# Attention stage of a decoder layer: every step with a q projection also gets one quarter of a u tile, and u is made by halves of the positions

## The chip, the cores and the metric

One core of one Trainium2 chip. The time is that of the device for one execution of the whole kernel, in microseconds (us), as the median of several runs. A profile of one execution shows each engine: PE (TensorE matmul; PEld is its weight load), DVE (VectorE), ACT (ScalarE), POOL (GpSimd) and SP (SyncE, which here issues DMAs).

## The reference

One decoder layer in float32 for 1024 positions of width 1024. What matters here is the input projection and the two token mixers:

```
h = rmsnorm(x)
[q | k | v | u | s | gate_a | gate_b] = h @ w_in      # in the kernel: q, k, v, u (512 wide), v_s (512 wide)
A = sliding_window_attention(q, k, v)                  # 8 heads of 64, window 128, ALiBi, a sink per head
B = gelu(u) * (tril(W_s) @ rmsnorm(gelu(v_s)) + b)     # in chunks of 128 positions
x = x + (sigmoid(gate_a) * (A @ w_oa) + sigmoid(gate_b) * (B @ w_ob)) @ w_out
x = x + down(silu(conv_g) * conv_v)                    # conv of width 3 over up(rmsnorm(x)), 2 x 2816 wide
```

## The kernel before

A product in float32 is made of three matmuls of a reduced float32: each operand is split into a high part (a copy by ACT, `copy_hi`) and a low part (a subtraction by DVE or POOL), and `mm3` adds high x high, high x low and low x high (lines 93 to 95).

The kernel is written out in one order by hand: each engine works its instructions in the order in which the code issues them. The change is in the attention stage, a loop of 20 steps (`for n in range(20)`). Attention step n < 16 is half of the heads (n // 8) for one block of 128 queries (n % 8). Its parts are spread over the steps:

- step n: `s_mm` (PE, the scores, PSUM tile `sc`; lines 439, 442), `s_mask` (DVE, lines 457 and 458, tile `c`), `s_max` (DVE, lines 465 to 467)
- step n + 1: `s_exp` (ACT exponentials, DVE sum and reciprocal, lines 479 and 480, POOL product, line 481)
- step n + 2: `p_trans` (PE transposes, tile `pt`), `p_split` (ACT `ch`, DVE `cl` in line 496, and four POOL selects that part the two key blocks, lines 503 and 505)
- step n + 4: `pv_mm` (PE, tile `pv`), `pv_out` (ACT and DVE, line 530, into `ya`). After the last step of each half `ya` is stored by SP (line 533).

Between these parts PE gets filling work, two slots to a step, from the table `FILL`: `q` is the q projection of a later attention step (24 matmuls of 256 columns), `u` one of 16 chunks of the u projection (12 matmuls of 512 columns), and `v` one half of the v_s projection of 128 positions (24 matmuls of 256 columns). The first slot stands ahead of `p_trans`, the second behind it. There are 12 `q`, 16 `u` and 4 `v`.

u has four tiles of 128 channels and 1024 positions. A chunk takes two of the eight k slices for all positions, so four chunks fill one PSUM tile `pu` of two banks, which DVE then evacuates in one instruction of 1024 columns (line 679). `pu` and the score tiles `sc` come from the same pool `psA` with two buffers of two banks: while a `pu` is being filled, the scores have one buffer.

`WHEN` names the step at whose end the weights of a later part are split; POOL makes the low part (line 110 for u, line 193 for q and v_s: `wv` and `wvB`). In step 15 SP begins to load x again (`rows_again`, tile `xa`, line 617); the second four rows of it are loaded behind the stage, into the buffer that `ya` leaves. ACT scales them (`x_gain`, line 631). Behind the stage `v_phase` finishes v_s (tile `pvs`, weights `wvB`), takes its GELU on ACT and its norm on DVE, and mixes (tile `pm`, seeded by ACT in line 926 and evacuated by DVE in line 943).

Of the kernel before, what the change touches and what calls it, by code (L numbers as in the profile page):

```python
# [14 lines left out]
ALU = mybir.AluOpType  # L15
# [12 lines left out]

ROWS = (slice(0, 64), slice(64, 128))
X_AHEAD = 5  # L30
FILL = "qu|q|qu|qu|uu|q|qu|qu|q|qu|qu|qu|q|uu|u|u|uu|vv|v|v".split("|")
WHEN = {"u1": 0, "q0": 1, "q1": 2, "u2": 5, "u3": 9, "v0": 13, "v1": 14, "z0": 16, "z1": 17}


# [7 lines left out]
def body(ctx, tc, nc, a):  # L42
    L, H = slice(0, 512), slice(512, 1024)
# [11 lines left out]
    def Y(s, dt=R, shape=None):  # L55
        return big.tile(shape or [128, 4, 1024], dt, tag="Y", name=nm(s), bufs=7)
# [16 lines left out]
    def PS(s):  # L73
        if psum.get("next"):
            return psum["next"].pop(0).tile([128, 1024], F, tag="P", name=nm(s))
        pools_ = psum["P"]
        pools_.append(pools_.pop(0))
        return pools_[-1].tile([128, 1024], F, tag="P", name=nm(s))
# [12 lines left out]
    def mm3(out, wh, wl, mh, ml, first, last, **kw):  # L91

        nc.tensor.matmul(out, wh, mh, start=first, stop=False, **kw)  # L93
        nc.tensor.matmul(out, wh, ml, start=False, stop=False, **kw)  # L94
        nc.tensor.matmul(out, wl, mh, start=False, stop=last, **kw)  # L95
# [21 lines left out]
    rstd_b = base.tile([128, 1024], F, name="rstd_b")  # L117
# [61 lines left out]
    def hx(j, k, c):  # L179

        h = c.start // 512
        return xq[k // 4][h][:, j, k % 4, c.start - 512 * h:c.stop - 512 * h]
# [44 lines left out]
    for k in range(8):  # L227
# [8 lines left out]
        for s in range(8):  # L236
            o = pkv[s // 4][:, (s % 4) * 256:(s % 4 + 1) * 256]
            c = slice(s * 128, (s + 1) * 128)
# [24 lines left out]
    def q_proj(n):  # L263
        half, b = divmod(n, 8)
        w = wq[half]
        p = PH("pq")[:, 0:256]
        c = slice(b * 128, (b + 1) * 128)
        for k in range(8):
            mm3(p, hx(0, k, c), hx(1, k, c), w[:, 0, k, :], w[:, 1, k, :], k == 0, k == 7)
        st[("pq", n)] = p  # L270
# [155 lines left out]
    uT = Y("uT", F)  # L426


    def s_mm(n):
        b = n % 8  # L430
        qs = st.pop(("qT", n))
        p = PS("sc")
        k0 = max(b - 1, 0) * 128
        ks = slice(k0, k0 + 256)
        for t2 in range(2):
            c = slice(t2 * 128, (t2 + 1) * 128)
            o = [p[:, (2 * g + t2) * 256:(2 * g + t2 + 1) * 256] for g in range(2)]
            for g in range(2):
                nc.tensor.matmul(o[g], qs[:, g, c], kTh[:, g, ks], start=t2 == 0, stop=False,
                                 skip_group_check=True)  # L440
            for g in range(2):
                nc.tensor.matmul(o[g], qs[:, g, c], kTl[:, g, ks], start=False, stop=True,
                                 skip_group_check=True)
        st[("ps", n)] = p.rearrange("p (h k) -> p h k", k=256)

    def s_mask(n):

        half, b = divmod(n, 8)
        p4 = st.pop(("ps", n))
        hs = slice(4 * half, 4 * half + 4)  # L450
        c = tm.tile([128, 4, 128], F, tag="c", name=nm("c"), bufs=3)
        if b == 0:
            nc.vector.tensor_tensor(c, p4[:, :, 0:128], ali[:, hs, :], op=ALU.add)
            nc.gpsimd.affine_select(out=c, in_=c, pattern=[[0, 4], [-1, 128]], compare_op=ALU.is_ge,
                                    fill=NEG, base=0, channel_multiplier=1)
        else:
            nc.vector.copy_predicated(p4[:, :, 128:256], msk, p4[:, :, 0:128])
            nc.vector.tensor_tensor(c, p4[:, :, 128:256], ali[:, hs, :], op=ALU.add)
        st[("c0", n)] = c

    def s_max(n):
        hs = slice(4 * (n // 8), 4 * (n // 8) + 4)
        c = st.pop(("c0", n))
        sm = tm.tile([128, 4, 4], F, tag="sm", name=nm("sm"), bufs=3)
        nc.vector.tensor_reduce(sm[:, 0, :], c, axis=AX.X, op=ALU.max)
        nc.vector.scalar_tensor_tensor(sm[:, 0, :], sm[:, 0, :], -1.0, nsink[:, hs], op0=ALU.mult, op1=ALU.min)
        nc.vector.tensor_tensor(sm[:, 2, :], sink_b[:, hs], sm[:, 0, :], op=ALU.add)
        st[("c", n)] = (c, sm)
# [3 lines left out]
    def s_exp(n):  # L472
        c, sm = st[("c", n)]
        m, den, es = sm[:, 0, :], sm[:, 1, :], sm[:, 2, :]
        for i in range(4):
            last_exp[0] = nc.scalar.activation(c[:, i, :], c[:, i, :], AF.Exp, bias=m[:, i:i + 1],
                                               accum_out=den[:, i:i + 1])
        nc.scalar.activation(es, es, AF.Exp)
        nc.vector.tensor_tensor(den, den, es, op=ALU.add)
        nc.vector.reciprocal(den, den)  # L480
        nc.gpsimd.tensor_tensor(c, c, den.unsqueeze(2).to_broadcast([128, 4, 128]), op=ALU.mult)
# [28 lines left out]
    def pv_mm(n):  # L510
        parts = st.pop(("p", n))
        p = PH("pv")
        ops = [(part[2], part[j]) for j in (0, 1) for part in parts[::-1]]
        for i, (kb, w) in enumerate(ops):
            for g in range(2):
                o = p[:, g * 256:(g + 1) * 256].rearrange("p (h q) -> p h q", q=128)
                nc.tensor.matmul(o, vhl[:, kb, g, :], w[:, 2 * g:2 * g + 2, :], start=i == 0 and g == 0,  # L517
                                 stop=i == len(ops) - 1, skip_group_check=True)
        st[("pv", n)] = p.rearrange("p (g h q) -> p g h q", g=2, q=128)
# [15 lines left out]
    ust = {("w", 0): tuple(u_next)}  # L535

    def u_chunk(i):
        t, j = divmod(i, 4)
        if j == 0:
            ust["p"] = PS("pu")  # L540
        p, (wh, wl) = ust["p"], ust[("w", t)]
        for k in (2 * j, 2 * j + 1):
            for h in range(2):
                c = slice(h * 512, (h + 1) * 512)
                mm3(p[:, c], wh[:, k, :], wl[:, k, :], hx(0, k, c), hx(1, k, c), k == 0, k == 7)
        return t if j == 3 else None

    n_q, n_u, n_v, u_done = [4], [0], [0], []
    pvs = {}

    def v_half(s, h):
        if h == 0:
            pvs[s] = PS("pvs")[:, 0:512] if s < 2 else PH("pvs")
        c = slice(s * 128, (s + 1) * 128)
        for k in range(8):
            mm3(pvs[s][:, 256 * h:256 * h + 256], hx(0, k, c), hx(1, k, c), wv[h][:, 0, k, :],
                wv[h][:, 1, k, :], h == 0 and k == 0, k == 7, skip_group_check=True)

    def filler(n, i):

        kind = FILL[n][i:i + 1]
        if kind == "q":
            q_proj(n_q[0])
            n_q[0] += 1
            return [n_q[0] - 1]
        if kind == "v":
            v_half(n_v[0], 0)
            n_v[0] += 1
        if kind == "u":
            t = u_chunk(n_u[0])  # L570
            n_u[0] += 1
            if t is not None:
                u_done.append((t, ust["p"]))
        return []

    wv = []
# [36 lines left out]
    def rows_again(r):  # L613

        t = Y("xa", F)
        for k in range(4):
            nc.sync.dma_start(t[:, k, :], a["xw"][4 * r + k, :, 257:1281])
        xr_raw.append(t)
# [24 lines left out]

    assert "".join(FILL).count("u") == 16 and "".join(FILL).count("q") == 12
    man = tc.manual_schedule()
    man.__enter__()
    for n in range(20):
        if n < 16:
            s_mm(n)
            s_mask(n)  # L650
        if 0 <= n - 1 < 16:
            s_exp(n - 1)
        if n < 16:
            s_max(n)
        if 0 <= n - 4 < 16:
            pv_mm(n - 4)
        q_new = filler(n, 0)
        if 0 <= n - 2 < 16:
            p_trans(n - 2)
        filler(n, 1)  # L660
        if 0 <= n - 4 < 16:
            pv_out(n - 4)
        for q in q_new:
            q_sq(q)
            q_ms(q)
        if 0 <= n - 2 < 16:
            p_split(n - 2)
        weights(n)
        if n == 15:
            rows_again(0)  # L670
        if n == 17:
            x_gain(0, (0, 1))
        if n == 18:
            x_gain(0, (2, 3))
            x_sums((0, 1), True)
        if n == 19:
            x_sums((2, 3), True)
        for t, p in u_done:
            nc.vector.tensor_tensor(uT[:, t, :], p, rstd_b, op=ALU.mult)
        u_done.clear()  # L680
        if n + 2 < 16:
            q_trans(n + 2)
            q_split(n + 2)
        for q in [3] + q_new if n == 0 else q_new:
            q_norm(q)
# [1360 lines left out]
```

## Time and profile before

| | us |
|---|---|
| three runs | 1184.26, 1184.44, 1184.85 |
| median | 1184.44 |
| span of the profiled execution, first to last instruction | 1183.5 |
| median less span (launch and end of an execution) | 0.9 |
| PE busy | 1170.3 (99% of the span) |
| attention stage, 48.93 to 182.10 | 133.17 |
| of which PE busy | 130.07 |

The profiled execution's own time is listed only as its span; what lies around it is 0.9 us, if it ran like the median. PE is busy for nearly the whole span, so the kernel's time is the time of its matmuls plus the waits of PE.

### The profile page before, as it was taken

What the parts mean: (1) busy time and instruction counts of PE and PEld (TensorE: products, weight loads), DVE (VectorE), ACT (ScalarE), POOL (GpSimd) and SP (SyncE); (2) the same over time, 40 slices, a digit from 0 to 9 for tenths busy, and PEclk for the clock granted to TensorE, in tenths of its full rate; (3) what the DMA queues carried; (4) which work ended last, traced back from release to release, by engine and by line L of the source; (5) the groups of instructions that cost most, each with busy time, mean ns of one, the idle gap of its engine ahead of it and who ended that gap; (6) DMA issues with size and microseconds to landing.
All of it is one profiled execution on the core that took longest, in us unless ns stands there. A gap on an engine that the chain in (4) does not pass through costs nothing.

```text
span 1183.5 us, 15928 instructions
## 1 busy us (share of the span) xinstructions
PE 1170.3 (99%) x5842; PEld 990.4 (84%) x5842; DVE 874.5 (74%) x1037; ACT 566.5 (48%) x878; POOL 631.8 (53%) x435
## 2 busy tenths in 40 slices
PE   8999999999999999999999999999999999999998
PEld 8989989988888878888878888888888888888887
DVE  7798975743536776678788788877888797875674
ACT  8555667644336653335444443444444445425331
POOL 2467685488884764444867677776767541000000
PEclk9999999999999999999999999999999999999999
DMA  7110136157556654454545445455555268975471
GB/s 272 37 55 19 54 130 228 56 168 239 161 160 204 233 193 154 146 176 132 138 129 169 118 149 152 142 141 134 166 137 160 72 219 287 365 232 196 155 231 67
DMA packets 80942, 188.66 MB, mean 159 GB/s; under 512 B 9184, under 2 KB 16864, under 8 KB 80736
## 3 DMA queue, kind: packets, MB, share of 16 engines
q1 hardware_dynamic: 73008, 167.58, 40.7%
q0 software_dynamic: 7456, 15.73, 8.0%
q10 hardware_dynamic: 400, 4.33, 1.1%
q8 instruction: 46, 0.75, 0.3%
q14 instruction: 32, 0.26, 0.1%
HBM read 146.97 MB, written 49.02 MB: 166 GB/s over the span
## 4 chain that ended last, share of the span: by engine, by line
PE 82%; DVE 4%; POOL 3%; ACT 2%; issue 2%; DMA 1%; DVEq 0%; POOLq 0%; SPq 0%; ACTq 0%
PE pz L1060 50%; PE pd L1855 10%; PE pdy L1855 8%; PE px L95 2%; PE px L93 2%; PE px L94 2%; PE pu L95 1%; PE pu L93 1%; PE pu L94 1%; PE pv L517 1%; PE pq L93 1%; PE pq L95 1%; PE pq L94 1%; DVE xa L621 1%; DMA lq<-wup 0%
## 5 line engine op out<-in xcount | busy, mean ns | idle before, releaser
L1060 PE MATMUL pz<-T,qh 128*128 128x512 f32 x472 | 145.6, 390 | 0.0
L1060 PE MATMUL pz<-B,ph 128*128 128x512 f32 x352 | 109.7, 393 | 0.7 <-ACT x L1695 0.7
L1060 PEld LDWEIGHTS pz<-T,qh 128*128 128x128 f32 x472 | 88.4, 188 | 18.6 <-ACT u L885 0.3
L1019 POOL TENSOR_TENSOR pl<-lp,ph 128x1024 fp32r<-128x1024 f32 x30 | 73.2, 2439 | 52.9 <-ACT ph L89 52.9
L1060 PE MATMUL pz<-T,ql 128*128 128x512 f32 x236 | 91.8, 389 | 0.0
L1019 POOL TENSOR_TENSOR ql<-lq,qh 128x1024 fp32r<-128x1024 f32 x30 | 76.8, 2559 | 9.1 <-ACT qh L89 9.1
L1060 PEld LDWEIGHTS pz<-B,ph 128*128 128x128 f32 x352 | 65.1, 188 | 16.7 <-ACT x L1695 3.8
L1078 DVE TENSOR_TENSOR pz<-pz,rstd_b 128x1024 f32<-128x1024 f32 x60 | 73.9, 1232 | 4.6 <-ACT rstd_b L143 2.5
L1060 PE MATMUL pz<-T,s3h 128*128 128x512 f32 x232 | 71.4, 389 | 0.0
L1060 PE MATMUL pz<-y,wjh 128*128 128x512 f32 x224 | 69.5, 391 | 0.6 <-POOL y L1233 0.3
L1060 PE MATMUL pz<-B,pl 128*128 128x512 f32 x176 | 68.6, 390 | 0.0
L1855 PE MATMUL pd<-bh,ah 128*128 128x512 f32 x176 | 68.5, 389 | 0.0
L1855 PE MATMUL pd<-bl,ah 128*128 128x512 f32 x176 | 68.5, 389 | 0.0
L1855 PE MATMUL pd<-bh,al 128*128 128x512 f32 x176 | 68.5, 389 | 0.0
L1060 PE MATMUL pz<-T,AX 128*128 128x512 f32 x264 | 63.4, 389 | 0.0
L1060 PE MATMUL pz<-B,AX 128*128 128x512 f32 x264 | 63.4, 389 | 0.0
L1019 POOL TENSOR_TENSOR s3l<-lq,s3h 128x512 fp32r<-128x512 f32 x20 | 26.0, 1298 | 62.3 <-ACT s3h L89 62.3
L1060 PEld LDWEIGHTS pz<-T,AX 128*128 128x128 f32 x264 | 49.5, 188 | 10.3
L1060 PEld LDWEIGHTS pz<-B,AX 128*128 128x128 f32 x264 | 49.6, 188 | 10.3
L89 ACT ACTIVATE AX<-lr 128x1024 fp32r<-128x1024 f32 x22 | 23.4, 1063 | 70.9 <-POOL lr L621 70.9
L621 DVE TENSOR_TENSOR pz<-pz,u 128x512 f32<-128x512 f32 x37 | 25.9, 700 | 42.5 <-ACT u L1072 36.2
L1550 DVE SCALAR_TENSOR_TENSOR tg<-pz,cp,tg 128x1023 f32<-128x1023 f32 (+1 forms) x44 | 56.2, 1278 | 0.8
(359 smaller groups left out, 3597.6 us busy)
## 6 DMA issues: line engine op xcount, KB each, us to landing
lp<-wup SPq DMA_DIRECT2D x22, 512.0 KB, 3.8
lq<-wup SPq DMA_DIRECT2D x22, 512.0 KB, 4.2
ra<-wdown SPq DMA_DIRECT2D x44, 256.0 KB, 4.9
b<-T SPq DMA_DIRECT2D x44, 256.0 KB, 3.5
lq<-wup POOLq DMA_DIRECT2D x42, 256.0 KB, 5.3
B<-tv SPq DMA_DIRECT2D x33, 256.0 KB, 2.0
T<-tt SPq DMA_DIRECT2D x33, 256.0 KB, 2.1
b<-B SPq DMA_DIRECT2D x33, 256.0 KB, 3.0
```

What stands on the lines that cost most here:

```text
L89: return nc.scalar.activation(dst, src, AF.Copy, scale=scale)
L93: nc.tensor.matmul(out, wh, mh, start=first, stop=False, **kw)
L94: nc.tensor.matmul(out, wh, ml, start=False, stop=False, **kw)
L95: nc.tensor.matmul(out, wl, mh, start=False, stop=last, **kw)
L517: nc.tensor.matmul(o, vhl[:, kb, g, :], w[:, 2 * g:2 * g + 2, :], start=i == 0 and g == 0, stop=i == len(ops) - 1, skip_group_check=True)
L621: eng.tensor_tensor(out, x, y, op=op)
L1019: nc.gpsimd.tensor_tensor(l, r, h.bitcast(F), op=ALU.subtract)
L1060: nc.tensor.matmul(o, p[:, k, :], m, start=not more and k == 0 and j == 0, stop=k == nk - 1 and j == 2, skip_group_check=True)
L1078: nc.vector.tensor_tensor(z, z, rstd_b, op=ALU.mult)
L1550: nc.vector.scalar_tensor_tensor(t[:, j:], p[:, 0:1024 - j], cw[:, ci, 2 - j:3 - j], t[:, j:], op0=ALU.mult, op1=ALU.add)
L1855: nc.tensor.matmul(o[d], p[:, k - k0, m], q[:, k - k0, :], start=new and k == 0 and j == 0, stop=k == HK - 1 and j == 2, skip_group_check= ...
```

## The change

`FILL` is rewritten: steps 0 to 11 all get `qu`, steps 12 to 15 one `u` each, steps 16 and 17 one `v` each, step 18 `vv` and step 19 nothing. A chunk of u now takes four of the eight k slices for 512 positions, so two chunks fill one bank; the pairs go through the first and the second 512 positions of each tile. One `pu` tile of two banks is held from the first chunk to the sixteenth, and each filled half is evacuated by an instruction of 512 columns while the other half is being filled.

```diff
-FILL = "qu|q|qu|qu|uu|q|qu|qu|q|qu|qu|qu|q|uu|u|u|uu|vv|v|v".split("|")
+FILL = "qu|qu|qu|qu|qu|qu|qu|qu|qu|qu|qu|qu|u|u|u|u|v|v|vv|".split("|")
...
     def u_chunk(i):
-        t, j = divmod(i, 4)
-        if j == 0:
+
+        t, h, j = i // 4, i // 2 % 2, i % 2
+        if i == 0:
             ust["p"] = PS("pu")
-        p, (wh, wl) = ust["p"], ust[("w", t)]
-        for k in (2 * j, 2 * j + 1):
-            for h in range(2):
-                c = slice(h * 512, (h + 1) * 512)
-                mm3(p[:, c], wh[:, k, :], wl[:, k, :], hx(0, k, c), hx(1, k, c), k == 0, k == 7)
-        return t if j == 3 else None
+        wh, wl = ust[("w", t)]
+        c = (L, H)[h]
+        p = ust["p"][:, c]
+        for k in range(4 * j, 4 * j + 4):
+            mm3(p, wh[:, k, :], wl[:, k, :], hx(0, k, c), hx(1, k, c), k == 0, k == 7)
+        return (t, c, p) if j else None
...
         if kind == "u":
-            t = u_chunk(n_u[0])
+            u = u_chunk(n_u[0])
             n_u[0] += 1
-            if t is not None:
-                u_done.append((t, ust["p"]))
+            if u:
+                u_done.append(u)
+            if n_u[0] == 16:
+                del ust["p"]
...
-        for t, p in u_done:
-            nc.vector.tensor_tensor(uT[:, t, :], p, rstd_b, op=ALU.mult)
+        for t, c, p in u_done:
+            nc.vector.tensor_tensor(uT[:, t, c], p, rstd_b[:, c], op=ALU.mult)
```

On PE, step 13 of the program before, from the end of its `pv` to the scores of step 14 (a run of like matmuls is left out at each line of dots; `pqt` is the transposed q of a later step):

```order
L517 MATMUL pv_1951<-cl_1818,vhl 128x256 x2
L93 MATMUL pu_1691<-x_5_118,wuh_1191 128x512
...
L487 MATMUL pt_1972<-ident,c_1738 128x128 x4
L93 MATMUL pu_1691<-x_5_118,wuh_1191 128x512
...
L295 MATMUL pqt_2010<-ident,qr_1925 128x128 x2
L439 MATMUL sc_2018<-kT_107,qs_1920 128x256 x2
```

The same step of the changed program:

```order
L517 MATMUL pv_1989<-cl_1876,vhl 128x256 x2
L93 MATMUL pu_735<-x_5_118,wuh_1670 128x512
...
L487 MATMUL pt_2010<-ident,c_1796 128x128 x4
L295 MATMUL pqt_2036<-ident,qr_1894 128x128 x2
L439 MATMUL sc_2044<-kT_107,qs_1960 128x256 x2
```

The second chunk of u has gone from this step to an earlier one, and the matmuls follow each other from `pt` to the scores of the next step.

On PE, the end of the stage before, from the `pv` of attention step 14 to the first matmul of `v_phase` (the one with `wvB`):

```order
L517 MATMUL pv_2306<-cl_2210,vhl 128x256 x2
L93 MATMUL pvs_2315<-wv_2004,x_3_116 128x256
...
L517 MATMUL pv_2349<-cl_2293,vhl 128x256 x2
L93 MATMUL pvs_2358<-wv_2004,x_3_116 128x256
...
L93 MATMUL pvs_2232<-wvB_2219,x_3_116 128x256
```

And in the changed program:

```order
L517 MATMUL pv_2307<-cl_2241,vhl 128x256 x2
L93 MATMUL pvs_2316<-wv_2030,x_3_116 128x256
...
L93 MATMUL pvs_2341<-wv_2030,x_3_116 128x256
...
L517 MATMUL pv_2375<-cl_2294,vhl 128x256 x2
L93 MATMUL pvs_2201<-wvB_2246,x_3_116 128x256
```

Both `v` of the end stand ahead of the `pv` of attention step 15 now, and none stands between it and `v_phase`.

## Rows read from the trace of the kernel before

A row of a stretch gives its length, then the busy us (and instructions) of PE, PEld, DVE, ACT and POOL, PE's granted clock, the DMA share and GB/s. A timeline's row gives start us, duration us and the instruction.

**Rows 1.** The profile's page: the span, and each engine's busy share.
```profile
span 1183.5 us, 15928 instructions
PE 1170.3 (99%) x5842; PEld 990.4 (84%) x5842; DVE 874.5 (74%) x1037; ACT 566.5 (48%) x878; POOL 631.8 (53%) x435
```

**Rows 2.** The attention stage in one stretch: us and busy us (instructions) by engine.
```profile
48.93:182.10 133.17, 130.07 (x920) 119.10 (x918) 113.36 (x240) 82.69 (x256) 92.01 (x99) 1.00 0.18 62
```

**Rows 3.** Timeline of PE: start us, duration us, instruction, [idle before it <-releaser].
```profile
83.05 0.47 PE L439 MATMUL sc<-kT,qs 128*128 128x256 f32 x2 [0.41 <-DVE uT L679]
179.02 0.51 PE L517 MATMUL pv<-cl,vhl 128*128 128x256 f32 x2 [0.54 <-POOL cl L505]
```

**Rows 4.** Timeline of PE: first score matmul of steps 1, 3, 4, 10, 12, 14, 15, then the next phase.
```profile
55.69 0.48 PE L439 MATMUL sc<-kT,qs 128*128 128x256 f32 x2
67.61 0.48 PE L439 MATMUL sc<-kT,qs 128*128 128x256 f32 x2
74.77 0.48 PE L439 MATMUL sc<-kT,qs 128*128 128x256 f32 x2
119.05 0.48 PE L439 MATMUL sc<-kT,qs 128*128 128x256 f32 x2
135.09 0.48 PE L439 MATMUL sc<-kT,qs 128*128 128x256 f32 x2
148.60 0.48 PE L439 MATMUL sc<-kT,qs 128*128 128x256 f32 x2
153.66 0.48 PE L439 MATMUL sc<-kT,qs 128*128 128x256 f32 x2
182.10 0.28 PE L93 MATMUL pvs<-wvB,x 128*128 128x256 f32 x1
```

**Rows 5.** Groups of DVE instructions by line in the stage: xcount | busy us, mean ns.
```profile
L458 DVE TENSOR_TENSOR c<-sc,ali 128x512 f32<-128x512 f32 x14 | 9.7, 691 | 0.6
L679 DVE TENSOR_TENSOR uT<-pu,rstd_b 128x1024 f32<-128x1024 f32 x4 | 4.9, 1215 | 0.0
```

**Rows 6.** Timeline of DVE in steps 12 to 14.
```profile
137.48 0.69 DVE L457 COPY_PREDICATED sc<-msk,sc 128x512 f32<-128x512 uint8 x1
144.06 0.69 DVE L457 COPY_PREDICATED sc<-msk,sc 128x512 f32<-128x512 uint8 x1
148.58 0.69 DVE L496 TENSOR_TENSOR cl<-pt,ch 128x512 fp32r<-128x512 f32 x1
152.66 1.08 DVE L479 TENSOR_TENSOR sm<-sm 128x4 f32<-128x4 f32 x1
```

**Rows 7.** Timeline of POOL at the end of the stage.
```profile
151.30 2.43 POOL L193 TENSOR_TENSOR wv<-v,wv 128x1024 fp32r<-128x1024 f32 x1
172.56 0.64 POOL L505 TENSOR_SCALAR_AFFINE_SELECT cl<-cl 128x512 fp32r<-128x512 f32 x1
```

**Rows 8.** SyncE's and ScalarE's timelines behind the stage.
```profile
181.28 0.80 SPq L533 DMA_DIRECT2D ya<-ya  x2
191.11 2.18 ACT L631 ACTIVATE xa<-xa,cp 128x1024 f32<-128x1024 f32 x2
```

**Rows 9.** The reload of x (tile xa), two first issues and their landing times.
```profile
L617 SPq DMA_DIRECT2D xa<-xw x2: 333/378/423, 185.6 to 186.0; - x2
DMA to landing us min/median/max: 3.6/4.7/5.7
```

**Rows 10.** Behind the stage: a link of the chain that ended last; PE's timeline.
```profile
191.21 2.08 ACT xa L631 x2
...
218.26 0.39 PE L93 MATMUL pm<-wgh,vsh 128*128 128x256 f32 x1 [0.52 <-ACT pm L926]
```

**Rows 11.** Kernel start: a PE wait, then two stretches with granted clock (third number from the end).
```profile
6.30 0.38 PE L93 MATMUL pkv<-wkv,x 128*128 128x256 f32 x1 [1.89 <-ACT x L89]
...
5.00:10.00 5.00, 3.64 (x17) 3.03 (x18) 3.24 (x7) 4.01 (x9) 0.00 (x0) 0.82 0.96 353
10.00:15.00 5.00, 5.00 (x38) 5.00 (x38) 5.00 (x11) 5.00 (x11) 0.00 (x0) 0.84 1.03 399
```


## The prediction

> **What bounds the kernel now.** I read the page first: PE is busy 99% of a span of 1183.5 us [rows 1], so time can only come from, or go into, PE's waits. Then the attention stage alone, from the first score matmul (48.93 us) to the first matmul that uses the second half of the w_v weights (182.10 us): 133.17 us with 130.07 busy [rows 2], so 3.10 us of it are idle. The waits of PE in that stage are small and of two kinds [rows 3]: in the steps that follow a step without a `u`, it waits a few tenths for DVE (0.41 us for the 1024-column evacuation `uT`, for instance), and near the end it waits for POOL, for the selects that cut the probabilities before the `pv` matmuls (0.54 us, tile `cl`). Last, the chain behind the stage: at 218.26 us PE waits 0.52 us for ScalarE's `pm` [rows 10], and the chain of waits that led there leaves PE for ScalarE and DVE well before, with the scaling of x at 191.21 us as one link of it [rows 10]. So there PE has no spare time to give: what ScalarE loses at 191 us, PE loses at 218 us.
>
> **The change part by part.**
>
> *Matmuls.* The same ones, in another order. No PE time is added or removed.
>
> *Steps 0 to 11 become uniform ("qu").* Such a step takes 8.02 us: steps 10 and 11 lie between 119.05 and 135.09 [rows 4]. Without its `pv` it takes 7.16 us, as step 3 does (67.61 to 74.77). Step 1 begins at 55.69 us as before. Steps 1 to 3 then take 3 x 7.16, less some 0.4 for the transposes that step 1 lacks (an estimate: 4 of its 50-odd matmuls), 21.1 us; step 4, with half a `pv`, 7.6; steps 5 to 11, 7 x 8.02 = 56.1. So step 12 begins at 55.7 + 21.1 + 7.6 + 56.1 = 140.5 us with no wait on the way, where it begins at 135.09 now with less work behind it. I cost these steps at no wait: steps 10 and 11 already are of this form, with one score buffer free, and they show none.
>
> *One score buffer all the time.* The score matmuls of a step need the mask and add of the step before (DVE, 0.69 each [rows 5, 6]) to be done. At least 4 us of other PE work lie between them even in a step with a single `u` (5.06 us from 148.60 to 153.66, less about 1 for the scores [rows 4]). Cost nothing; from the other side, 0.41 us at each place where DVE is late [rows 3].
>
> *Evacuations.* Eight of 512 columns in place of four of 1024. The 1024 form takes 1.215 us, a 512-column add out of PSUM 0.691 [rows 5]: 8 x 0.691 - 4 x 1.215 = 0.7 us more DVE time, spread over seven quiet steps and step 15. Nothing on the path, and the 0.41 us wait for the long one goes.
>
> *The end of the stage, which decides.* Steps 12 to 15 now have one `u` and nothing else, about 5 us of PE each, and steps 16 to 19 have `v`, `v`, `vv` and nothing. The work of DVE and POOL per step stays. So I follow POOL. In step 12 DVE starts its mask at step start + 2.39 us (135.09 to 137.48 [rows 4, 6]); this is the same afterwards. One step of DVE is 6.58 us there (137.48 to 144.06), of which 1.07 belong to a q (its three small instructions): 5.5 afterwards. From that mask to the `cl` subtraction in the same step are 4.52 us (144.06 to 148.58), with about 0.6 of waits for POOL: 3.9 to 4.5 afterwards. From this subtraction to the POOL instruction that makes the low part of `wv` are 2.72 us (148.58 to 151.30 [rows 6, 7]). So this first `wv` instruction starts at 2.4 + 5.5 + 3.9 + 2.7 = 14.5 us behind step 12's start, at 155.0 us (upper bound 155.6, from the 4.5; lower 154.0, if DVE were not behind PE at all). From there the order of POOL and DVE is the same in both kernels up to the end of the `cl` select of attention step 14: 151.30 to 172.56 + 0.64, 21.9 us. In that stretch POOL hardly rests and PE is early with all that it hands over, so I carry the 21.9 over whole: `cl` of step 14 is ready at 176.9 us. Then PE has the last pair of `pv` (0.4), two `v` (2.73 each: 182.10 - 179.02 - 0.35 [rows 3, 4]) and the `pv` of step 15 (0.9): the next phase begins at 176.9 + 0.4 + 5.5 + 0.9 = 183.7 us, **1.6 us later** than the 182.10 of now. The waits that went in the early steps come back, and more, as waits for POOL in steps 16 to 18.
>
> One instruction in that chain is worth a look. DVE's small product `sm` (L479) takes 1.08 us and ends at 153.74, just when POOL's `wv` instruction (151.30 + 2.43) ends [rows 6, 7]; I take it as held until then, as part of the 21.9. By my times POOL is first there by some 0.8 us (14.5 against about 15.3 us behind step 12). If DVE came first, what is held now would not be: 14.5 + 2.43 - 15.3 = 1.6 us would go out of the chain (a rival, below). The Trainium skill, page "SBUF — State Buffer", section "Who interferes with whom", has such a rule: a DVE instruction with two SBUF inputs and a GpSimd instruction that reads SBUF exclude each other for the whole instruction, and whichever issues first has its way. By that rule the trace agrees for the one order that it shows.
>
> *What hangs on the `pv` of step 15.* Now a `v` (2.73 us) lies between it and the next phase; afterwards none. Its result goes through ScalarE and DVE to `ya`, and SyncE stores `ya` (181.28 us [rows 8], 2.26 us behind the last pair at 179.02 [rows 3]). Behind that store, on the same queue, stands the reload of four rows of x (tile `xa`), which takes the buffer of `ya` and so waits until the store has landed; its first two issues are at 185.6 and 186.0 us and land 3.6 and 5.7 us later [rows 9], at 189.2 and 191.7. Afterwards the last pair is at 183.7 - 0.35 = 183.35, the store at 185.6, 4.3 us later, so the second row of x lands at 196.0. ScalarE scales the two rows from 191.11 us on, 1.09 each [rows 8]; moved by 1.6 us it would want the second row at 191.11 + 1.09 + 1.6 = 193.8. It waits **2.2 us**, and everything behind it on ScalarE with it: the GELU of the third v chunk, for which DVE waits, and so on up to `pm` and PE at 218 us, where there is no slack [rows 10]. Bounds: nothing, if the stores and loads land sooner on a freer queue; 3 us, if all four rows matter.
>
> **Sum.** 1.6 + 2.2 = +3.8 us on the profiled span of 1183.5 us, 1187.3; the runs' median, 1184.44, stands 0.9 above that span: **1188.2 us**.
>
> **The rivals.**
> - *POOL does not hold PE (faster).* From step 15 on (153.66 to 182.10 [rows 4], 28.4 us with its waits) PE now has three `u` and four `v` left. Afterwards it has as many left from step 13 on, at 140.5 + 4.7 = 145.2 us, with the scores, `pv` and transposes of two more steps, about 4.6 us. With the waits of now the stage would end at 145.2 + 28.4 + 4.6 = 178.2 us, 3.9 early: 1180.5 us. That needs `cl` of step 14 some 5.5 us sooner, so the first `wv` instruction by about 9 us behind step 12 instead of 14.5, or a chain of 16 us instead of 21.9. Against it: DVE alone needs 11.8 of the 14.5, and POOL is shown busy for nearly all of the chain. Chance 0.10.
> - *The x rows are hidden.* The stage ends 1.6 us later and nothing follows: 1186.0. For it: ScalarE's scaling is shown with no wait now, and the store meets a freer queue. Chance 0.21.
> - *DVE first.* `sm` starts ahead of POOL's first `wv` instruction and is not held: 1.6 us leave the chain, the stage ends as now, and the lost cover of the `ya` store still costs 2.2: 1186.6. Chance 0.08.
> - *The clock falls.* At the kernel's start PE waited 1.89 us, and the granted clock then averaged 0.82 and 0.84 over two stretches of 5 us [rows 11]: it stood for a while at 1.2 instead of 2.4 GHz, at a cost of up to (0.18 + 0.16) x 5 = 1.7 us. In step 17 I expect some 3 us of waits for POOL in pieces. A like fall would cost about 1.5 us: 1189.7. Page "TensorE: Matmul & The Clock Gate", section "What's actually happening", of the Trainium skill gives an idle array the lower clock. The short waits of the stage now leave it at 1.00 [rows 2], so I hold it unlikely. Chance 0.11.
>
> **How the numbers follow.** My forecast has a chance of 0.50; the time is its own. A measurement of this kernel tells about 0.2%, 2.4 us, from no change: 1182.1 to 1186.8 is "same". Faster is the first rival, 0.10; same are the second and third, 0.29; slower the forecast and the last, 0.61. The range leaves out the first rival, and takes in the bounds of the forecast (155.0 down to 154.0 with 2.2, or 155.6 with 3 us: 1187.2 to 1189.6), the middle rivals with the lower start, and most of the last: 1185.0 to 1190.5. The slower cases' own range is 1187.0 to 1190.5.
>
> **What would show it.** Steps 1 to 11 without PE waits and step 12 at 140.5 us; the first `wv` instruction of POOL at 155.0; PE waits for POOL's `cl` of 1 to 3 us at the `pv` of steps 16, 17 and 18; the next phase at 183.7; the `ya` store at 185.6 and a ScalarE wait of some 2 us ahead of the second scaled row; the matmul `pm` near 222 us. I am wrong if step 12 starts later (waits that I don't see in the uniform steps), if POOL passes its chain in less than 21 us, or if the rows of x land in time.

## The result, and the profile after

The changed kernel takes 1189.57 us (median of 5 runs, 1189.46 to 1190.59), the one before 1184.26 us beside it. The ratio is 1.0046, with a 95% interval of 1.0034 to 1.0058: 5.3 us slower.

The page of the changed kernel answers to [rows 1]: the busy times are those of before, the span is 4.2 us longer.

```profile
span 1187.7 us, 15936 instructions
PE 1170.6 (99%) x5842; PEld 991.6 (83%) x5842; DVE 872.5 (73%) x1041; ACT 566.7 (48%) x878; POOL 631.1 (53%) x435
```

Three stretches of it: the attention stage (as [rows 2]), from there to the first product behind v_phase (`pz`), and the rest.

```profile
48.73:183.41 134.68, 130.87 (x919) 120.24 (x918) 110.14 (x240) 80.94 (x253) 90.51 (x99) 0.99 0.17 60
183.41:225.38 41.97, 37.95 (x326) 37.55 (x325) 27.72 (x42) 30.78 (x50) 15.95 (x15) 1.00 0.54 188
225.38:1187.70 962.32, 957.42 (x4258) 790.84 (x4256) 698.79 (x691) 423.21 (x518) 509.92 (x305) 1.00 0.55 170
```

And the last two of the kernel before:

```profile
182.10:219.75 37.65, 37.13 (x326) 36.93 (x325) 25.05 (x38) 28.68 (x47) 14.98 (x14) 1.00 0.58 203
219.75:1183.50 963.75, 958.16 (x4258) 790.65 (x4256) 700.18 (x691) 423.24 (x518) 510.05 (x305) 1.00 0.54 170
```

The stage took 1.5 us more and began 0.2 sooner, so the next phase begins 1.3 us later. Most is lost **behind** the stage, where nothing was edited: 41.97 us in place of 37.65, 4.3 more. The first `pz` is 5.6 us late. From there to the end the two profiled executions differ by 1.4 us the other way; in all fourteen profiles of this study that part takes 962 to 965 us. So runs are compared by where `pz` begins, and their medians beside it.

PE's timeline shows where it waits in the stage (as [rows 3], [rows 4]) and behind it (as [rows 10]):

```profile
140.28 0.48 PE L439 MATMUL sc<-kT,qs 128*128 128x256 f32 x2
...
153.44 0.50 PE L93 MATMUL pu<-x,wuh 128*128 128x512 f32 x1 [0.95 <-DVE uT L682]
...
168.53 0.50 PE L517 MATMUL pv<-ch,vhl 128*128 128x256 f32 x2 [0.92 <-POOL ch L505]
170.74 0.80 PE L517 MATMUL pv<-cl,vhl 128*128 128x256 f32 x2 [1.13 <-POOL cl L505]
...
202.48 0.38 PE L93 MATMUL pvs<-wv,x 128*128 128x256 f32 x1 [2.56 <-DVE vg L763]
...
223.90 0.38 PE L93 MATMUL pm<-wgh,vsh 128*128 128x256 f32 x1 [1.46 <-ACT pm L929]
```

POOL and DVE at the end of the stage (as [rows 6] and [rows 7]): the chain from `wv` to the `cl` of attention step 14 runs from 154.81 to 176.63.

```profile
154.81 2.43 POOL L193 TENSOR_TENSOR wv<-v,wv 128x1024 fp32r<-128x1024 f32 x1
155.72 1.54 DVE L479 TENSOR_TENSOR sm<-sm 128x4 f32<-128x4 f32 x1
175.99 0.64 POOL L505 TENSOR_SCALAR_AFFINE_SELECT cl<-cl 128x512 fp32r<-128x512 f32 x1
```

SP and ACT behind it (as [rows 8] and [rows 9]): the store of `ya`, the reload of `xa`, its landing times, and ACT waiting twice for its rows.

```profile
185.88 0.80 SPq L533 DMA_DIRECT2D ya<-ya  x2
190.26 2.73 SPq L620 DMA_DIRECT2D xa<-xw  x4
DMA to landing us min/median/max: 6.3/7.9/8.9
196.70 1.15 ACT L634 ACTIVATE xa<-xa,cp 128x1024 f32<-128x1024 f32 x1 [4.14 <-DMA xa<-xw]
198.35 1.15 ACT L634 ACTIVATE xa<-xa,cp 128x1024 f32<-128x1024 f32 x1 [0.49 <-DMA xa<-xw]
```

Line numbers behind line 573 of the kernel before are 3 higher in the changed one. The time stands 1.7 to 1.8 us above the span in every run of either kernel whose span is known; so the profiled execution of before, whose span was 1183.5, took about 1185.2 us, not the median.

### The profile page after: what moved, and what is told of

Its sections match the earlier page's. It is cut to its first block, busy times and chain, and to the rows that moved or that the text cites. A ratio compares the mean times of both kernels' runs of the same rounds, so it can differ in the third digit from the quotient of the medians.

```text
span 1187.7 us, 15936 instructions
## 1 busy us (share of the span) xinstructions
PE 1170.6 (99%) x5842; PEld 991.6 (83%) x5842; DVE 872.5 (73%) x1041; ACT 566.7 (48%) x878; POOL 631.1 (53%) x435
## 4 chain that ended last, share of the span: by engine, by line
PE 90%; DVE 4%; DMA 2%; POOL 1%; issue 1%; ACT 1%; SPq 0%; DVEq 0%; POOLq 0%; ACTq 0%
PE pz L1063 53%; PE pd L1858 10%; PE pdy L1858 8%; PE px L95 2%; PE px L94 2%; PE px L93 2%; PE pq L93 1%; PE pq L95 1%; PE pq L94 1%; PE pu L95 1%; PE pu L93 1%; PE pu L94 1%; PE pv L517 1%; DVE xa L624 1%; DMA xa<-xw 1%
## 5 line engine op out<-in xcount | busy, mean ns | idle before, releaser
L1553 DVE SCALAR_TENSOR_TENSOR tv<-pz,cp,tv 128x1023 f32<-128x1023 f32 (+1 forms) x44 | 56.2, 1278 | 0.8
```

Of the source, the lines that this page charges most:

```text
L1553: nc.vector.scalar_tensor_tensor(t[:, j:], p[:, 0:1024 - j], cw[:, ci, 2 - j:3 - j], t[:, j:], op0=ALU.mult, op1=ALU.add)
```

## The experiments

Each run was timed against the kernel before on the same chip (its medians there: 1184.4 to 1184.7).

| run | us | ratio to before, 95% | first `pz` |
|---|---|---|---|
| before | 1184.3 | | 219.75 |
| changed | 1189.57 | 1.0034 to 1.0058 | 225.38 |
| halves_old_table | 1188.86 | 1.0024 to 1.0050 | 224.84 |
| quarters_new_table | 1191.25 | 1.0044 to 1.0071 | 225.74 |
| halves_old_held | 1184.13 | 0.9990 to 1.0007 | 219.54 |
| wv_early | 1187.28 | 1.0008 to 1.0030 | 222.67 |
| gain_later | 1192.54 | 1.0054 to 1.0080 | 226.07 |
| ya_early | 1185.30 | 1.0004 to 1.0021 | 220.63 |
| v_behind | 1191.67 | 1.0046 to 1.0073 | 227.17 |
| wb_later | 1189.52 | 1.0027 to 1.0053 | 225.91 |
| wb_first_later | 1188.80 | 1.0024 to 1.0048 | 224.75 |
| tail_relief | 1188.00 | 1.0018 to 1.0041 | 222.61 |
| tail_ya_first | 1184.48 | 0.9991 to 1.0009 | 217.81 |
| quarters_ya_first | 1184.93 | 0.9996 to 1.0014 | 218.43 |

### Which half of the change: the table, or the form of u

**halves_old_table**: the changed kernel with the `FILL` of before.

> The u tiles by halves of positions with 512-column evacuations and one held pu tile, but FILL as in the kernel before: only the form of u is changed. Theory (the loss is made by the table, that is by POOL's and DVE's chain in steps 13 to 18 and by the late store of ya, and one score buffer costs nothing): 1184.6 us, between 1184.0 and 1185.5; the next phase starts at 182 to 183 us as before, and ACT waits for no row of xa. Rival (the halves themselves cost, through the single score buffer of all steps or through eight evacuations in place of four): 1187 us or more, with waits of PE's scores for DVE's u evacuation in the early steps.

Measured: 1188.86 us. My theory fell: the halves alone lose 4 us. But neither cause that the rival named is there. It is one wait, in step 16. DVE's and PE's timelines:

```profile
148.88 0.68 DVE L682 TENSOR_TENSOR uT<-pu,rstd_b 128x512 f32<-128x512 f32 x1
163.77 0.68 DVE L682 TENSOR_TENSOR uT<-pu,rstd_b 128x512 f32<-128x512 f32 x1
164.50 0.80 PE L93 MATMUL pu<-x,wuh 128*128 128x512 f32 x1 [4.92 <-DVE uT L682]
```

This matmul begins chunk 14, the second half of the last u tile. That half had last been evacuated at 148.88, 15 us before. The evacuation at 163.77, with whose end the wait ends, is that of the **other** half, chunks 12 and 13. Both halves are slices of one tile `pu`, and in this trace a write into one half waits for the read of the other. So the second half can't be filled while the first is being evacuated, as the change meant it. The windows around it show what the wait costs on top (the number behind the five engines is PE's granted clock):

```profile
159.00:164.40 5.40, 0.58 (x5) 0.38 (x4) 5.29 (x8) 2.81 (x12) 4.34 (x5) 0.84 0.33 108
164.40:169.80 5.40, 5.30 (x14) 4.14 (x15) 1.16 (x5) 1.06 (x1) 5.40 (x6) 0.52 0.92 377
169.80:172.00 2.20, 2.20 (x14) 1.85 (x13) 0.69 (x1) 1.55 (x2) 1.17 (x3) 1.00 0.26 35
```

After 4.9 us in which PE had nothing to do the clock stood near its lower level, 1.2 GHz, for about 5 us, and the twelve matmuls took 5.2 us where they take 2.75 elsewhere.

**halves_old_held**: the same, but the evacuation of the first half of the last tile is held back until the second is full.

```diff
+        if n_u[0] < 14 or n_u[0] == 16:
-        for t, c, p in u_done:
-            nc.vector.tensor_tensor(uT[:, t, c], p, rstd_b[:, c], op=ALU.mult)
-        u_done.clear()
+            for t, c, p in u_done:
+                nc.vector.tensor_tensor(uT[:, t, c], p, rstd_b[:, c], op=ALU.mult)
+            u_done.clear()
```

> The halves with the FILL of the kernel before, as in the run halves_old_table, but the first half of the last u tile is evacuated together with its second half behind chunk 15, so no chunk follows an evacuation of the other half of pu closely. Theory (a chunk that begins one half of pu waits for the evacuation of the other half, since both are one tile; the idle 4.9 us and the 2.4 us of matmuls at half clock behind it made that run slow): no pu matmul waits, the granted clock stays at 1.00 around 165 us, 1184.0 us, between 1183.2 and 1185.2. Rival (the chunk waited for the evacuation of its own half, or the halves cost elsewhere): a wait of pu of several us at step 16 stays, 1187.5 us or more.

Measured: 1184.13 us, the time of the kernel before; no `pu` matmul waits, and the clock stays.

```profile
158.00:172.00 14.00, 13.46 (x92) 11.94 (x91) 9.69 (x17) 8.03 (x20) 12.81 (x14) 1.00 0.56 205
```

So the halves cost nothing of themselves, nor does one score buffer in all steps. What costs is that the halves are not apart for the waits, where an evacuation is followed closely by the next chunk. (Two separate tiles for the halves were not tried.) In the changed kernel the same wait is the 0.95 us at 153.44.

**quarters_new_table**: the kernel before with the new `FILL` alone.

> The new FILL with the u tiles as in the kernel before (two k slices for all positions, evacuated by 1024 columns, two buffers shared with the scores). Theory (the table alone makes the loss): 1189.5 us, between 1188.5 and 1190.5, with POOL's first wv near 155, ACT waiting 4 us for the rows of xa, and the first wvB matmul near 183.5. Rival (the halves make the loss): 1184 to 1186 us.

Measured: 1191.25 us, 0.75 above my interval, and on the theory's side: the table alone makes a loss of this size. The stage goes as expected too: the first `wv` at 154.92, the first `wvB` matmul at 183.54, and ACT waits 4.19 + 0.62 us for rows of `xa`. Whether the halves take some of it back can't be told, since the intervals of this run and of the changed kernel overlap.

### The end of the stage

**wv_early**: POOL splits the first v_s weights three steps sooner.

```diff
-WHEN = {"u1": 0, "q0": 1, "q1": 2, "u2": 5, "u3": 9, "v0": 13, "v1": 14, "z0": 16, "z1": 17}
+WHEN = {"u1": 0, "q0": 1, "q1": 2, "u2": 5, "u3": 9, "v0": 10, "v1": 11, "z0": 16, "z1": 17}
```

> The changed kernel with the two splits of the first v_s weights (wv) at the ends of steps 10 and 11 instead of 13 and 14. Theory (these two POOL instructions at 154.8 and 162.8 us lengthen POOL's chain to the selects of attention steps 13 and 14): PE's waits of about 5 us between 153 and 177 us go mostly, the first wvB matmul starts near 179.5 us (178.5 to 182) instead of 183.4, the store of ya and the rows of xa come as much earlier: 1184.0 us, between 1182.0 and 1186.0. Rival (the thin filler at the end leaves PE without work however early the weights are split, since the scores, exponentials and transposes of the last steps set the pace): the next phase stays within 1 us of 183.4 and the time is 1188.5 us or more.

Measured: 1187.28 us, 1.3 above my interval; runs from 1184.8 to 1191.3. In the profile no wait for POOL is left in the stage and the first `wvB` matmul starts at 180.91, 2.5 us sooner, so the POOL chain is shown as what set the end. Two things kept the rest. In the stage, PE waits longer for the other half of `pu`, and the matmuls behind it run at the lower clock, so that the end is 1.4 us later than the 179.5 expected. And behind the stage the rows of `xa` still come late for ACT, which wants them sooner as well: from the first `wvB` matmul to `pz` it takes 41.8 us, 42.0 in the changed kernel. PE's and ACT's timelines:

```profile
155.65 0.80 PE L93 MATMUL pu<-x,wuh 128*128 128x512 f32 x1 [2.61 <-DVE uT L682]
...
193.18 1.15 ACT L634 ACTIVATE xa<-xa,cp 128x1024 f32<-128x1024 f32 x1 [3.15 <-DMA xa<-xw]
...
199.72 0.58 PE L93 MATMUL pvs<-wv,x 128*128 128x256 f32 x1 [2.31 <-DVE vg L763]
```

### The reload of xa

**ya_early**: only the store of `ya`, and so the reload, is moved ahead.

```diff
-        if b == 7:
+        if b == 6 and half == 1 or b == 7 and half == 0:
             for t in (2 * half, 2 * half + 1):
-                nc.sync.dma_start(d_ya[t], ya[:, t, :])
+                if half == 0:
+                    nc.sync.dma_start(d_ya[t], ya[:, t, :])
+                else:
+                    nc.sync.dma_start(d_ya[t][:, 0:896], ya[:, t, 0:896])
+                    nc.sync.dma_start(d_ya[t][:, 896:1024], ya[:, t, 768:896])
```

> The changed kernel with the second half of ya stored one step earlier, before its last block is written (the last 128 columns of that half are therefore stored from the block ahead of it: the output is not the reference's). Only the start of the reload of xa moves: from 190.3 us to about 186, when ya's last block has been written. Theory (the late rows of xa cost PE 2.6 us at the first use of vg and about 1 us at pm): the first row lands between 189.5 and 192.4, ACT wants it at 192.6 and waits for none; PE waits for no vg and about 0.5 at pm: 1186.1 us, between 1185.5 and 1187.0, with the stage's end at 183.4 as before. Rival (ACT's wait is hidden, the five us are lost elsewhere): 1189.5 us, not under 1188.8.

Measured: 1185.30 us, about 4 less than the changed kernel. SP asks for `xa` at 186.03 and ACT scales its rows without a wait:

```profile
186.03 1.98 SPq L624 DMA_DIRECT2D xa<-xw  x4
191.95 2.18 ACT L638 ACTIVATE xa<-xa,cp 128x1024 f32<-128x1024 f32 x2
```

PE waits for no `vg` and 0.52 at `pm`, though the stage ends at 182.92, 0.5 us sooner than in the changed kernel but not as early as in the one before. The late reload is thus the larger part of the loss, about four of five us.

**gain_later**: ACT's scaling and DVE's sums that need it stand one step of v_phase later.

```diff
-        2: lambda: (x_sums((0,), False), g_left[0].sum_s4(), g_left[0].sum_f3()),
-        3: lambda: (x_sums((1,), False), g_left[0].first_s3()),
-        4: lambda: (x_sums((3,), False), g_left[0].first_s4()),
+        2: lambda: (g_left[0].sum_s4(), g_left[0].sum_f3()),
+        3: lambda: (x_sums((0,), False), g_left[0].first_s3()),
+        4: lambda: (x_sums((1,), False), g_left[0].first_s4()),
...
-        1: lambda: x_gain(1, (0, 1)),
-        2: lambda: x_gain(1, (2, 3)),
-        3: lambda: (x_sums((2,), False), sgu_seed(0, 0, psA), sgu_seed(1, 0, psA)),
+        2: lambda: x_gain(1, (0, 1)),
+        3: lambda: (x_gain(1, (2, 3)), sgu_seed(0, 0, psA), sgu_seed(1, 0, psA)),
+        4: lambda: x_sums((2, 3), False),
```

> The changed kernel with ACT's scaling of the second four rows of xa moved one step of v_phase back (behind the GELU of v_s 2 and 3 instead of 1 and 2), and DVE's sums that need them one step back too. Theory (the late rows of xa hold ACT and through it the GELU, vg and PE): the GELU of v_s 2 starts near 192.6 us instead of 199.4, PE's wait of 2.6 us for vg is gone and that at pm is about 0.5 instead of 1.5: 1186.1 us, between 1185.5 and 1187.2, the stage's end staying at 183.4. Rival (the end of the stage costs everything, and what ACT waits for the rows is hidden): 1189.5 us, no change.

Measured: 1192.54 us, 3 worse: a miss. The first part came true: ACT waits for no row, PE for no `vg`. But the sums that I moved put DVE behind at the end of v_phase; ACT waits for DVE's `vg`, and PE for ACT:

```profile
219.11 0.63 ACT L89 ACTIVATE vsh<-vg 128x512 fp32r<-128x512 f32 x1 [4.30 <-DVE vg L763]
...
223.35 0.58 PE L93 MATMUL pm<-wgh,vsh 128*128 128x256 f32 x1 [4.46 <-ACT pm L929]
```

The run replaced one wait by another, so its time says nothing on the first.

**v_behind**: a `v` behind the last `pv` again.

```diff
-FILL = "qu|qu|qu|qu|qu|qu|qu|qu|qu|qu|qu|qu|u|u|u|u|v|v|vv|".split("|")
+FILL = "qu|qu|qu|qu|qu|qu|qu|qu|qu|qu|qu|qu|u|u|u|u|v|v|v|v".split("|")
```

> The changed kernel with one v in each of the steps 16 to 19 instead of two in step 18, so that a v stands behind the pv of attention step 15 again. Theory by the trace of the changed kernel (POOL's selects set when this pv can start, and DVE's sums of x, held by POOL's wvB until 185.0 us, set when ya is complete): pv of step 15 waits for cl until 181.6, 1.8 us; the first wvB matmul starts at 185.3 instead of 183.4, the store of ya and the rows of xa come when they did, and PE's wait for vg shrinks by as much as the stage's end moved: 1189.6 us, between 1188.8 and 1190.6. Rival (the v behind the last pv is the cover that was lost, and gives it back): the store 2.7 us earlier, 1187 us or less.

Measured: 1191.67 us, 1 us above the theory's interval and 2 above the changed kernel, so the rival is out. The first `wvB` matmul starts at 184.5 (a `v` of 2.74 us begins at 181.77), 1.1 us later, and PE's wait for `vg` shrinks by as much, as the theory said. What it did not see is a new wait of PE for `vg` ahead of `pz`, 1.6 us. The last `pv` ends near 181.8 us, but `ya` is complete only at 185.6, since DVE stands in sums of x that overlap POOL's `wvB`. POOL's and DVE's timelines:

```profile
181.34 2.87 POOL L193 TENSOR_TENSOR wvB<-z,wvB 128x1024 fp32r<-128x1024 f32 x1
...
181.14 3.62 DVE L624 TENSOR_TENSOR xa<-xa 128x512 f32<-128x512 f32 x2
184.77 0.86 DVE L530 TENSOR_TENSOR ya<-pv,o 64x256 f32<-64x256 f32 x2
185.66 1.29 DVE L624 TENSOR_TENSOR xa<-xa 128x512 f32<-128x512 f32 x2
```

The pair of sums takes 3.62 us beside `wvB` and 1.29 without it. The Trainium skill, page "SBUF — State Buffer", section "Who interferes with whom", says that a DVE instruction that reads two SBUF operands and a GpSimd instruction that reads SBUF shut each other out; these rows agree.

**wb_later** and **wb_first_later** ask why the first row of `xa` landed 6.3 us after its issue, where it took 3.6 before [rows 9]. On another queue, ACT asks for two `wb` rows of 512 KB at 187.13 and 190.40 us; in the kernel before, the first of them stood 0.2 us behind the first row of `xa`. In the edits, s counts the steps of v_phase.

```diff
-            wb_copy(s)
+            if s != 1:
+                wb_copy(s)
+            if s == 2:
+                wb_copy(1)
```

> The changed kernel with the second wb transfer, which ACT issued at 190.40 us, 0.14 behind the first row of xa, moved behind the third one (past 200 us). Theory (the first row of xa landed 6.3 us after its issue instead of 3.6 because it shared the DMA engines with this wb and what was left of the one before): the rows land about 1.3 us earlier (512 KB at some 400 GB/s), ACT waits 2.5 to 3.5 us in place of 4.6, and the time is 1188.2 us, between 1187.2 and 1189.2. Rival (what is late is the issue alone, and sharing costs nothing): ACT waits 4.6 us as before and the time stays at 1189.5.

Measured: 1189.52 us, and ACT waits 4.26 us. The first row took 7.1 us, not less: the second `wb` was not it. The other run issues none at s = 0, the first at s = 1 and two at s = 2:

```diff
-            wb_copy(s)
+            if s < 3:
+                for j in ((), (0,), (1, 2))[s]:
+                    wb_copy(j)
+            else:
+                wb_copy(s)
```

> The changed kernel with the wb transfers of ACT one step later: none where ACT issued the first at 187.1 us (3.1 ahead of the first row of xa), the first where the second stood (190.4, 0.14 behind that row), the other two at the step after. The run wb_later moved the second one and the first row of xa came no earlier, so what is left that differs from the kernel before is the first wb: there it was issued 0.2 us behind the first row, which landed in 3.6 us. Theory (a wb issued ahead of the rows takes the DMA engines from them; one behind them doesn't): the first row lands 3.6 us after its issue, near 193.9, ACT waits 1.3 us in place of 4.6, PE waits for no vg: 1186.8 us, between 1186.0 and 1188.0. Rival (the rows land late for another reason, the rb load or the place in the time): ACT waits 4 us or more and the time stays above 1188.8.

Measured: 1188.80 us, above my interval; ACT's timeline:

```profile
194.86 1.16 ACT L634 ACTIVATE xa<-xa,cp 128x1024 f32<-128x1024 f32 x1 [2.26 <-DMA xa<-xw]
197.27 1.15 ACT L634 ACTIVATE xa<-xa,cp 128x1024 f32<-128x1024 f32 x1 [1.25 <-DMA xa<-xw]
```

The first row came 1.8 us sooner, ACT waited 3.5 us in all instead of 4.6, and the time fell by less than its spread. The first row's landing in all fourteen profiles points the same way: in the six whose first `wb` was issued 0.2 to 0.6 us behind the first row of `xa`, this row took 3.4 to 3.7 us; in the seven where it was issued 1.8 to 3.1 us ahead, 4.5 to 7.1. A transfer issued some us ahead of the rows does delay the first of them, but the second stays late in wb_first_later. What else delays them is open.

### Mending it

**tail_relief**: the edits of wv_early, halves_old_held and v_behind together on the changed kernel.

> The changed kernel with three edits: the wv splits at steps 10 and 11 (as in the run wv_early), the last u tile evacuated only when both its halves are full, and one v in each of the steps 16 to 19. Theory (in the run wv_early PE lost 2.6 us for the evacuation of the other half of pu and 1.4 us to half clock behind it, and the reload of xa was still late): without these waits the first wvB matmul starts between 177 and 180.5 us, pv of attention step 15 stands one v ahead of it, so ACT waits at most 2 us for xa: 1181.8 us, between 1180.0 and 1184.0, faster than both kernels. Rival (the chain of exponentials, transposes and selects of the last steps sets the end, whatever PE has to do): the first wvB matmul not before 181.5 us, 1185 us or more.

Measured: 1188.00 us: a miss, though the first `wvB` matmul came at 179.52, within what I expected and 2.6 us sooner than in the kernel before. All of it and more was lost behind that. PE's, ACT's and SP's timelines:

```profile
176.44 0.50 PE L517 MATMUL pv<-cl,vhl 128*128 128x256 f32 x2 [0.20 <-POOL cl L505]
179.52 0.28 PE L93 MATMUL pvs<-wvB,x 128*128 128x256 f32 x1
...
176.03 2.19 ACT L634 ACTIVATE xa<-xa,cp 128x1024 f32<-128x1024 f32 x2
178.24 0.75 ACT L527 COPY o<-pv 64x256 f32<-64x256 f32 x2
...
180.84 0.80 SPq L533 DMA_DIRECT2D ya<-ya  x2
185.21 3.30 SPq L620 DMA_DIRECT2D xa<-xw  x4
...
193.79 1.16 ACT L634 ACTIVATE xa<-xa,cp 128x1024 f32<-128x1024 f32 x1 [2.55 <-DMA xa<-xw]
```

The last `pv` was done near 176.8, where the last `v` began, but its copy on ACT stood behind the scaling of the first `xa`, and `ya` was stored 4.1 us later. (The next expectation speaks of 5 us that PE won. That takes the start of this `v`, 176.78, for the start of the next phase. In the kernel before, too, a `v` stands behind the last `pv`; like for like, PE won 2.6.)

**tail_ya_first**: tail_relief, with that scaling and the sums behind the output of step 15.

```diff
-        if n == 18:
-            x_gain(0, (2, 3))
-            x_sums((0, 1), True)
         if n == 19:
-            x_sums((2, 3), True)
+            x_gain(0, (2, 3))
+            x_sums((0, 1, 2, 3), True)
```

> The kernel of the run tail_relief with one more edit: ACT's scaling of the last two rows of the first xa and DVE's sums of the first two rows stand behind the output of attention step 15 instead of ahead of it. In tail_relief this pv started at 175.0 us, but ACT copied it out only at 178.2, behind the scaling, and DVE added it only at 179.95, behind sums that POOL's wvB held; so ya was stored at 180.8 and the second xa asked for at 185.2. Theory (the reload of xa, not the attention steps, is what took back the 5 us that PE won there): ya is stored near 177.7, xa asked for near 182, its rows are there when ACT wants them at 188.5, PE waits for no vg and less than 0.5 at pm: 1181.0 us, between 1179.5 and 1183.5, faster than both kernels. Rival (the rows still come late, or the sums moved behind become late themselves): 1185 us or more.

Measured: 1184.48 us (1182.98 to 1186.00), level with the kernel before and 5 below the changed one, but not the 1181 that I expected. The store went out at 177.56, ACT waits for no row:

```profile
177.56 0.80 SPq L533 DMA_DIRECT2D ya<-ya  x2
181.90 1.89 SPq L620 DMA_DIRECT2D xa<-xw  x4
187.41 2.18 ACT L634 ACTIVATE xa<-xa,cp 128x1024 f32<-128x1024 f32 x2
```

`pz` starts at 217.81 in its profile, 1.9 us before that of the kernel before and behind a new wait for DVE's `vg`:

```profile
217.81 0.73 PE L1062 MATMUL pz<-x,ph 128*128 128x512 f32 x2 [1.59 <-DVE vg L762]
```

All four runs with one `v` in each of the last four steps have this wait (1.58 to 1.62 us, v_behind first), and no other run has it. It takes back part of what was won; what makes it is open. The medians show no gain at all, and where the rest went is open too.

**quarters_ya_first**: the same with the u tiles of before.

> The run tail_ya_first with the u tiles of the kernel before (two k slices for all positions, one evacuation of 1024 columns, buffers shared with the scores): the table, the early wv, a v in each of the last four steps and the output of attention step 15 ahead of the scaling. Theory (the form of u is worth little once nothing waits for it): within 1 us of tail_ya_first, about 1181.5 us. Rival (the halves are what lets the uniform steps run without waits): 1183 us or more, with waits of the scores for the evacuation of u.

Measured: 1184.93 us: 0.45 from the other, as the theory said, with the absolute time missed alike. By its time the rival (1183 or more) would fit as well, but the waits that it names are not there: no score matmul waits for an evacuation of u. No version here beats the kernel before by more than can be measured.

## Why the prediction was right, and where its terms were off

The prediction was 1188.2 us (1185.0 to 1190.5), slower; measured 1189.57.

- *Steps 0 to 11 uniform, no waits, step 12 at 140.5 us.* Right: 140.28, no PE wait in steps 1 to 11. (One reading was off, without weight in the sum: the wait of 0.41 us at 83.05 [rows 3] follows step 4, which has two `u`, not a step without one.)
- *One score buffer and eight evacuations cost nothing.* Right by halves_old_held. What I did not see is the wait of a chunk for the evacuation of the other half of the same tile: 0.95 us at 153.44. I had taken the halves as apart.
- *The first `wv` at 155.0, chain of 21.9 us, `cl` at 176.9, next phase at 183.7 (+1.6).* 154.81, 21.8, 176.63, 183.41 (+1.3). PE's single waits were smaller than the 1 to 3 us that I named: the largest for POOL are 1.13 and 0.92, both in step 17, and none is marked in step 18. The wait for the other half did not add to the sum, since the POOL chain sets the end: quarters_new_table doesn't have this wait, and its next phase starts at 183.54. That this chain does set it, wv_early showed. POOL's `wv` was ahead of DVE's `sm` (155.72), so the rival "DVE first" did not come about.
- *The store at 185.6 (+4.3); ACT waits 2.2 us, bounds 0 to 3.* The mechanism is right, as ya_early showed: without the late reload about 4 of the 5.3 us come back. The size is the step that failed: the store came at 185.88, and ACT waited 4.14 + 0.49 = 4.6 us. I carried the landing times of before over (3.6 and 5.7 us behind the first issue); the first row took 6.3.
- *All of ACT's wait reaches PE at `pm`.* Mostly, and the larger part sooner: PE lost 2.56 at `vg` and 0.9 more than before at `pm`, 3.5 of the 4.6 us.
- *`pm` near 222 us*: 223.90, against 218.26 [rows 10].
- *The clock falls (rival).* It did, for 3 us, behind PE's waits in step 17:

```profile
170.00:171.00 1.00, 0.26 (x1) 0.26 (x2) 0.00 (x0) 0.87 (x1) 1.00 (x3) 0.71 0.99 401
171.00:172.00 1.00, 1.00 (x6) 1.00 (x7) 0.22 (x1) 1.00 (x3) 1.00 (x2) 0.50 1.05 430
172.00:173.00 1.00, 1.00 (x6) 1.00 (x6) 0.47 (x1) 0.97 (x2) 1.00 (x1) 0.50 1.02 418
```

But it cost the stage little: in gain_later and wb_later, whose clock stayed at 1.00 there, the first `wvB` matmul starts at 183.12 and 183.79, against 183.41. There PE waits for POOL's selects in step 18 instead (0.28, 0.20 and 0.20 us in gain_later).

- *The base.* I added 0.9 us to the span; it is about 1.7. This does not explain the miss, since the forecast goes from median to median: +3.8 us, where 5.1 (from 1184.44) or 5.3 (from 1184.26) were measured. By spans, 1187.3 was forecast and 1187.7 measured, but that is luck: `pz` came 5.6 us late, not 3.8, and the rest of this execution happened to be 1.4 us shorter than in the profile of before.

## What to carry to other kernels

Spreading filler evenly over steps that hardly wait takes it from the end, where another engine's chain then shows; price the end of a stage first, and with it every transfer that hangs on its last output. Two halves of one tile need not be two buffers, and here were not: look at which evacuation a matmul waits for, and hold it back (splitting the tile was not tried here). When transfers move in time, don't carry their landing times over, and read which instructions stand ahead of the last output on each engine.

## What the runs showed of the hardware

- The clock was down for about 5 us after PE had idled 4.9 us (halves_old_table), and in the changed kernel for 3 us, behind four windows of 1 us, from 167 us on, in which PE was busy 0.61, 0.47, 0.53 and 0.26; it came back while PE worked without a gap. The Trainium skill, page "TensorE: Matmul & The Clock Gate", section "What's actually happening", says that idling brings the lower clock. These falls agree. But in gain_later PE was busy for the same 1.86 of the 4 us from 167 on, and the clock stayed; what decides between the two, these rows of gain_later (granted clock 1.00 in both) don't show:

```profile
167.00:171.00 4.00, 1.86 (x10) 1.24 (x10) 2.09 (x6) 1.61 (x4) 3.48 (x5) 1.00 1.02 415
171.00:174.00 3.00, 3.00 (x28) 2.87 (x26) 1.54 (x3) 2.05 (x4) 3.00 (x3) 1.00 0.66 270
```

- The first of four 512 KB rows, asked for on one queue, landed 3.6 us after its issue in the kernel before and 4.5 in wb_first_later, in both with a 512 KB transfer of another queue issued just behind it, and 6.3 in the changed kernel, where one more such transfer had been issued 3.1 us ahead of it. In wb_later, with the one ahead (by 2.4 us) and none just behind, it took 7.1.
